# A transformer layer on one core: attention, gates and Fourier map ordered on every engine by one plan

## The chip, the cores and the metric

The kernel runs on one core of one Trainium2 chip. A core has a matrix engine (PE; its weight loads are listed as PEld), a vector engine (DVE), an activation engine (ACT), a general engine (POOL) and a queue engine (SP) that here only issues DMAs. Each engine takes its instructions in the order in which they stand in the program and waits at semaphores for the others. The metric is device time of the whole layer in microseconds (us), lower is better.

## The reference

One layer: a mixer of two branches (attention and a Fourier branch) merged by sigmoid gates, then a squared-ReLU MLP. All inputs are float32, 1024 latent tokens, 256 context tokens, width 1024, 8 heads.

```python
hx = modulate(rmsnorm(x, norm1_g[l]), sh1, sc1)          # hc: the same for the context
fx, qlx, kvlx, krx, gx = split_proj(hx @ w_in[l])        # 512 | 256 | 128 | 32 | 2 x 1024 gates
kx, vx = mla_kv(kvlx, krx, kv_norm_g[l], w_kvb[l], k_gain[l], rope)
qx = mla_q(qlx, q_norm_g[l], w_qb[l], q_gain[l], rope)
# 8 heads, 96 numbers for q and k, 64 for v; 1024 queries over 1024 + 256 keys
att_x = latent_attention(qx, jnp.concatenate([kx, kc], axis=1), jnp.concatenate([vx, vc], axis=1))
g = jax.nn.sigmoid(gx + b_gate)
y = g_f * (fourier_mix(fx) @ w_fourier) + g_a * (att_x @ w_mla_o)
x = x + g1 * (y @ w_out)
h2 = modulate(rmsnorm(x, norm2_g[l]), sh2, sc2)
x = x + g2 * jnp.square(jax.nn.relu(h2 @ w_up)) @ w_down
```

## The kernel before

Tokens lie along the free dimension in two halves of 512. A float32 product is made of three matmuls: each operand is split into a rounded high part (ACT copies it) and a low part (DVE subtracts), and PE multiplies high-high, high-low and low-high. So nearly every operand costs one ACT and one DVE instruction.

The program has three parts.

The **front**, up to the first head of attention: projections, norms, the q and k vectors of all heads (kept in DRAM), v, the Fourier transforms over positions, and the first 8 of 16 gate blocks. Each step is a task with an engine, an assumed duration, dependencies and buffers. `plan` (line 263) is a list scheduler: it takes the task that can start first by its assumed durations, and for equal starts the one with the smaller priority number. The 128 pieces of the first 8 gates (three matmuls each, `g_piece`) have the lowest rank and fill PE's gaps. All five engines issue in the plan's order. The front also holds 24 sums `ada_dot` that make later modulation numbers; 12 of them run on DVE at line 928, of low rank too. `first_head` makes q and k of head 0 and the row maxima of its first query half: 12 matmuls, 12 DVE maxima (line 1431), then a diagonal matrix of the negative maxima (line 1436, DVE) that PE turns into a row (`row`) and ACT copies under q, so that the score matmul subtracts the maximum.

**Attention** has 160 steps: 8 heads x 2 query halves x 10 key blocks. A step is three score matmuls (`score`), two exponentials on ACT (a float16 high part and a float32 one), a low part `pp` on DVE for each third step and on POOL else, and 4 + 4 float16 matmuls with v (`weigh`: 129 columns for the high part, 65 for the low one). The next head's q and k are loaded, multiplied by their norm on POOL (`hat`), split, and their row maxima made (`smax`, line 1529). The other 8 gates are spread over the steps (`gates_plan`), the Fourier map (`fmap_plan`) over the last 20 and beyond. Each action is filed with a time in steps (`at`), and `advance` makes them in order of time. Only PE is bound to that order (`manual_schedule(engines={PE})`); DVE, ACT, POOL and SP are ordered by the framework's own scheduler. The front's plan is written out in full before attention's first action. `k_tiles(1)`, which writes a row of ones into the second set of k tiles on POOL, and two small DVE products for later (`ax2`, `g1h`) stand between.

The **rest**, from the merge to the MLP, is a second plan, again ordered on all engines.

Buffers are rings: 58 of 2 KB per partition (`u`), 8 for short use (`t`), 5 for `pp`; in PSUM two banks each for maxima (`p0`), scores (`p1`), v products (`p2`), gates and Fourier map (`p4`).

Of the kernel before, what the change touches and what calls it, by code (L numbers as in the profile page):

```python
# [23 lines left out]
KB = 8  # L24
# [7 lines left out]
def hybrid_layer_kernel(ctx, tc, xT, ctxT, cvec, cctx, adaw, smalls, w_in4, w_in, w_qb, w_kvk, w_kvv, w_fo, w_f64,  # L32
# [216 lines left out]
    def lag(d, eng):  # L249
# [7 lines left out]
                              r"u2_|x_\d|c22_|c12_|c21_")  # L257

    def on_port(n):
        eng, dur = tasks[n][:2]  # L260
        return eng == "POOL" and dur > 0.3 or eng == "DVE" and not free_of_port.match(n)

    def plan(pre=None):
# [22 lines left out]
        while ready:  # L286
            best = None
            for n in ready:
                eng, dur, _, _, deps, new, _ = tasks[n]
                st = max([end[d] + lag(d, eng) for d in deps], default=0.0)  # L290
                st = max(st, free.get(eng, 0.0), free.get("port", 0.0) if on_port(n) else 0.0)
                want = {}
                for tag, _ in new:
                    want[tag] = want.get(tag, 0) + 1
                for tag, m in want.items():
                    if len(slots[tag]) < m:
                        break
# [681 lines left out]
    def c_add(j):  # L979
        tt(C["q", j][:, 0], C["q", j][:, 0], C["q", j][:, 1], ALU.add, nc.gpsimd)  # L980
# [63 lines left out]
    def alt_cast():  # L1044
        DT["a"] = Tm((1, 514), F32R)
# [196 lines left out]
    def g_piece(i, hf, k):  # L1242
        key = f"G{i}{hf}"

        def run():
# [73 lines left out]
    load("altl", 0.1, alt_load, ("q16",), (("t", "altr"),))  # L1319
    op("altc", "ACT", 0.55, alt_cast, ("altl",), (("t", "alta"),), ("altr",))  # L1320
# [75 lines left out]
    def first_head():  # L1396
        op("hk", "POOL", 3.0, lambda: k_tiles(0), ("ds1",), tuple(("u", f"hxk{i}") for i in range(6)))
# [11 lines left out]
        for c in range(2):  # L1409
# [7 lines left out]
            op(f"hqt{c}", "SP", 0.02, tiles, ("ds1",), (("u", f"hxq{c}h"), ("u", f"hxq{c}l")))  # L1417
# [1221 lines left out]
```

## Time and profile before

| | us |
|---|---|
| runs | 1485.41, 1482.95, 1488.93 (median 1485.41) |
| profiled execution | 1487.4 |
| its span (first to last instruction) | 1485.6 |
| front, to the first head's maxima | 0 to about 320 |
| end of the front and start of attention | about 320 to 364 |
| attention | about 339 to 707 |
| rest | from about 720 |
| PE busy | 1430.8 (96%) |
| DVE / ACT / POOL busy | 1117.8 (75%) / 789.0 (53%) / 346.4 (23%) |

Matmuls are pipelined, so PE counts as busy from the first start to the last end of a dense row. A stretch is full when the granted clock (PEclk) is 1.00 and matmuls follow without a gap, as in the rest (3245 matmuls in 763.6 us); a half clock shows as 0.50. The profile's rows name instructions by the program's tile names, as out<-in; line 79 is the matmul helper, 93 an elementwise helper, 99 the activation helper.

### The profile page before, as it was taken

To read this page: it belongs to the slowest core of one execution; us is meant where nothing else is said; L and a number is where in the kernel's file an instruction comes from. 1 tells how busy PE (TensorE), PEld (TensorE's weight loads), DVE (VectorE), ACT (ScalarE), POOL (GpSimd) and SP (SyncE) were. 2 spreads that over 40 slices of the span, in tenths; PEclk is the share of its full clock that TensorE was granted. 3 is DMA by queue.
4 is the path that set the end of the run, shared out by engine and by line. 5 is a ranking of instruction groups with operands and counts; after the bars stand their busy time and mean duration, and the time that the engine had idled before them with its cause. 6 is when DMAs were issued, how large, how long until landed. Compare 5 with 4: busy or idle time off the path is not lost. (4 is left out here: it accounts for less than half of the span.)

```text
span 1485.6 us, 20465 instructions
## 1 busy us (share of the span) xinstructions
PE 1430.8 (96%) x7208; PEld 1125.5 (76%) x7208; DVE 1117.8 (75%) x1763; ACT 789.0 (53%) x1287; POOL 346.4 (23%) x277
## 2 busy tenths in 40 slices
PE   8999999996999999999999999999999999999998
PEld 7767667874777777776887787888888788888887
DVE  4898786668776867786866888876666888877885
ACT  5654757653777777777433474444444443333431
POOL 0010653613554537355321200000000110100000
PEclk9999998997999999999999999999999999999999
DMA  9413455575222312213748556564444883536232
GB/s 339 160 45 129 149 169 169 179 227 172 65 85 76 91 49 80 68 50 105 246 146 276 164 175 207 199 227 156 151 140 154 288 288 120 199 100 206 92 127 100
DMA packets 103520, 229.09 MB, mean 154 GB/s; under 512 B 12765, under 2 KB 15877, under 8 KB 103418
## 3 DMA queue, kind: packets, MB, share of 16 engines
q1 hardware_dynamic: 103418, 227.80, 46.3%
q8 instruction: 56, 0.92, 0.3%
q14 instruction: 46, 0.38, 0.1%
HBM read 171.12 MB, written 56.61 MB: 153 GB/s over the span
## 5 line engine op out<-in xcount | busy, mean ns | idle before, releaser
L79 PE MATMUL ps<-u,wh 128*128 128x512 f32 (+1 forms) x1760 | 557.5, 398 | 2.2 <-DVE u L96 1.0
L79 PEld LDWEIGHTS ps<-u,wh 128*128 128x128 f32 x1760 | 326.8, 191 | 77.2 <-issue 4.0
L79 PE MATMUL ps<-u,wl 128*128 128x512 f32 (+2 forms) x880 | 344.6, 392 | 0.0
L79 PE MATMUL ps<-u,u 96*128 96x512 f32 (+4 forms) x862 | 250.6, 406 | 21.2 <-DVE mx L1529 8.9
L79 PEld LDWEIGHTS ps<-u,u 96*128 96x128 f32 (+3 forms) x862 | 158.3, 194 | 64.5 <-DVE mx L1529 14.0
L79 PEld LDWEIGHTS ps<-u,wl 128*128 128x128 f32 x880 | 167.6, 190 | 37.2
L93 POOL TENSOR_TENSOR u<-u,u 96x512 f32<-96x512 f32 (+1 forms) x34 | 52.0, 1536 | 530.6 <-DVE t L93 323.7
L99 ACT ACTIVATE wh<-wr 128x1024 fp32r<-128x1024 f32 (+1 forms) x108 | 94.6, 881 | 136.9 <-DMA wr<-d 103.0
L93 POOL TENSOR_TENSOR pp<-t,pp 128x512 f16<-128x512 f32 x106 | 126.1, 1192 | 144.9 <-ACT t L99 53.1
L79 PE MATMUL ps<-ab,pp 128*128 128x129 f16 (+2 forms) x1504 | 154.4, 238 | 4.9 <-ACT pp L99 2.8
L99 ACT ACTIVATE pp<-ps,lnps 128x512 f16<-128x512 f32 x160 | 109.4, 684 | 69.9 <-PE ps L79 68.4
L1529 DVE TENSOR_REDUCE mx<-ps 128x1 f32<-128x512 f32 (+1 forms) x180 | 105.2, 595 | 53.0 <-PE ps L79 52.0
L93 DVE TENSOR_TENSOR wl<-wr,wh 128x1024 fp32r<-128x1024 f32 (+1 forms) x108 | 125.7, 1169 | 18.8 <-ACT wh L99 18.6
L79 PE MATMUL ps<-u,ab 128*128 128x512 f32 (+4 forms) x516 | 120.8, 384 | 2.0 <-DVE t L1208 1.3
L93 DVE TENSOR_TENSOR u<-u,u 128x512 f32<-128x512 f32 (+5 forms) x139 | 106.0, 782 | 19.2 <-ACT u L99 16.7
L99 ACT ACTIVATE t<-ps 128x512 f32<-128x512 f32 (+6 forms) x102 | 52.7, 522 | 118.2 <-PE ps L79 107.6
L79 PEld LDWEIGHTS ps<-u,ab 128*128 128x128 f32 (+1 forms) x516 | 92.5, 189 | 24.6 <-DVE t L1208 2.2
L99 ACT ACTIVATE t<-ps,lnps 128x512 f32<-128x512 f32 x160 | 108.1, 681 | 0.0
L99 ACT ACTIVATE t<-t 128x512 f32<-128x512 f32 (+4 forms) x138 | 84.2, 619 | 44.3 <-DVE t L93 32.5
L99 ACT ACTIVATE u<-u 128x512 fp32r<-128x512 f32 (+4 forms) x120 | 72.0, 611 | 65.9 <-POOL u L93 35.1
L79 PE MATMUL ps<-ab,u 128*128 128x512 f32 x240 | 91.6, 395 | 0.0
L79 PE MATMUL ps<-wh,u 128*128 128x512 f32 x232 | 91.2, 396 | 0.0
(194 smaller groups left out, 2136.4 us busy)
## 6 DMA issues: line engine op xcount, KB each, us to landing
d<-t SPq DMA_DIRECT2D x135, 256.0 KB, 2.4
wr<-d SPq DMA_DIRECT2D x56, 512.0 KB, 3.5
wr<-in_w_up_dram SPq DMA_DIRECT2D x39, 512.0 KB, 4.9
u<-in_adaw_dram SPq DMA_DIRECT2D x64, 256.0 KB, 4.3
u<-in_w_dn_dram SPq DMA_DIRECT2D x64, 256.0 KB, 6.8
ab<-in_adaw_dram SPq DMA_DIRECT2D x24, 512.0 KB, 5.9
t<-d SPq DMA_DIRECT2D x48, 256.0 KB, 4.2
wr<-in_w_in_dram SPq DMA_DIRECT2D x22, 512.0 KB, 5.5
```

The costliest lines, as they stand in the source:

```text
L79: return nc.tensor.matmul(o, lhsT=l, rhs=r, start=start, stop=stop, **k)
L93: (eng or nc.vector).tensor_tensor(out=o, in0=a, in1=b, op=op)
L99: nc.scalar.activation(out=o, in_=i, func=f, **k)
L1529: nc.vector.reduce_max(out=x["mx"][:, qb, kc:kc + 1], in_=p[:, :n], axis=AX.X)
```

## The change

Attention, gates 8 to 15 and the Fourier map become tasks of the front's plan, which now orders all five engines up to the end of the Fourier map. The names of PE's tasks: `S_n` scores, `H_n` and `W_n` the products of the high and low parts with v, `mm` a maximum's matmul, `mr` the row of maxima, `gp` a gate piece, `fm` the Fourier map; `E_n`, `X_n` are the exponentials, `L_n` the low part, `red_m` a maximum, `md` the diagonal.

- These tasks are "late": their priorities are 1000 plus twice the step, and they do not lengthen the front's own chains. Equal starts go to the front's tasks first; what can start earlier goes earlier.
- `either` lets the plan choose DVE or POOL for a task: low parts, the multiplications of q and k, two sums of the Fourier map's weights and one of its result, four sums of the context's squares. Counted in the two programs, 50 instructions of 282 move from POOL to DVE: 20 low parts, 15 multiplications of q and k, 15 sums.
- The norms of k are loaded per block and no longer once per head (788 SP DMAs for 781). After the v products one `scalar_tensor_tensor` does what a `tensor_scalar` and a `tensor_tensor` did: 32 `tensor_scalar` go.
- `k_tiles(1)` is a task without a dependency on the modulation sums; `ax2` and `g1h` follow the plan.
- The one-row table `alt` of the position transform is loaded after the third Fourier block and not after the q vectors.
- The gates' and q/k tiles are tracked as buffers; PE's matmuls are the same in number and shape (8372 rows with weight loads).

```diff
     def plan(pre=None):
...
-                tail[n] = tasks[n][1] + max([depth(m) + lag(n, tasks[m][0]) for m in succ[n]], default=0.0)
+                tail[n] = tasks[n][1] + max([depth(m) + lag(n, tasks[m][0]) for m in succ[n] if m not in late_tasks],
+                                            default=0.0)
...
+                for eng, dur in either.get(n, (tasks[n][:2],)):
+                    st = max([end[d] + lag(d, eng) for d in deps], default=0.0)
+                    st = max(st, free.get(eng, 0.0), free.get("port", 0.0) if on_port(n, eng, dur) else 0.0)
...
+                        key = (st + (GAP if prio[n] >= 1e6 else 0.0), prio[n], st + dur)
...
-        op(f"gp{n}", "PE", 3 * M, run, (f"gp{n - 1}" if n else "F30b", f"G{i}l0", f"G{i}l1"),
+        n = KB * gseq.index((i, hf)) + k
+        s = GS + (n - 16 * NGB + 0.5) * (GE - GS) / (16 * (16 - NGB))
...
+        op(f"gp{n}", "PE", 3 * M, run, (f"gp{n - 1}" if n else "F30b", f"G{i}l0", f"G{i}l1",
+                                        *((f"S_{int(s) - GA}",) if s >= GA and n >= 16 * NGB else ())),
...
+           1e6 + n if n < 16 * NGB else P0 + W * s)
...
-    load("altl", 0.1, alt_load, ("q16",), (("t", "altr"),))
+    load("altl", 0.1, alt_load, ("F20b",), (("t", "altr"),))
...
-    order, ends = plan()
-    for t, fn in order:
-        at(t, fn)
-    with tc.manual_schedule(engines=MANUAL):
-        advance(1e6)
...
-    k_tiles(1)
...
+    def late(name, eng, dur, fn, deps=(), new=(), use=(), t=0.0):
+        late_tasks.add(name)
+        task(name, eng, dur, P0 + W * t, fn, *deps, new=new, use=use)
+
+    def late_any(name, dve, pool, fn, deps=(), new=(), use=(), t=0.0):
+
+        late(name, "DVE", dve, lambda: fn(nc.gpsimd if tasks[name][0] == "POOL" else nc.vector), deps, new, use, t)
+        either[name] = (("DVE", dve * SCALE["DVE"]), ("POOL", pool * SCALE["POOL"]))
...
+        late(f"S_{n}", "PE", 3 * M + 0.03, score,
+             (qdep(h, c, "l"), kdep(h, kc, "l"), "hsc" if n < 10 else f"mc{hc}", *((f"S_{n - 1}",) if n else ())),
+             (("p1", f"sp{n}"),), (f"qh{hc}h", f"qh{hc}l", f"kt{b}{kc}", f"kt{b}{3 + kc}"), n)
+        late(f"E_{n}", "ACT", 0.61, exp_h, (f"S_{n}",), (("pp", f"pp{n}"),), (f"sp{n}",), n + 0.3)
+        late(f"X_{n}", "ACT", 0.61, exp_f, (f"E_{n}",), (("t", f"pf{n}"),), (f"sp{n}",), n + 0.35)
+        late_any(f"L_{n}", 0.65, 1.16, lambda e: e.tensor_tensor(out=x["pp"][:, 1], in0=x["f"], in1=x["pp"][:, 0],
+                                                                 op=ALU.subtract),
+                 (f"X_{n}",), (), (f"pp{n}", f"pf{n}"), n + 0.9)
...
+    late("hk1", "POOL", 3.0, lambda: k_tiles(1), ("hk",), tuple(("u", f"kt1{i}") for i in range(6)), (), -8)
...
+    order, ends = plan()
+    with tc.manual_schedule(engines=MANUAL):
+        for _, fn in order:
+            fn()
+    stt(ax2, adam[:, 32:40], 1.0, sm[:, N2G:N2G + 8], ALU.add, ALU.mult)
+    nc.vector.tensor_scalar_mul(out=g1h, in0=adam[:, 16:24], scalar1=0.5)
```

**Where the order differs.** Place 1 is PE at the row of the first maxima (`onesr`) and the first scores. Before (`wh_3287`, `wl_3288` are gate weights, `u_2685` is k's third block, `u_2661` its first, `u_2683` q):

```order
L79 MATMUL ps_3306<-u_902,wh_3287 128x512
L79 MATMUL ps_3306<-u_903,wh_3287 128x512
L79 MATMUL ps_3306<-u_902,wl_3288 128x512
L79 MATMUL ps_3306<-u_907,wh_3287 128x512
L79 MATMUL ps_3198<-u_2685,u_2661 128x256
L79 MATMUL ps_3306<-u_908,wh_3287 128x512
L79 MATMUL ps_3306<-u_907,wl_3288 128x512
L79 MATMUL ps_3216<-t_3210,onesr 128x512
L79 MATMUL ps_3329<-u_2661,u_2683 128x512
L79 MATMUL ps_3329<-u_2662,u_2683 128x512
L79 MATMUL ps_3329<-u_2661,u_2686 128x512
```

Between the last maximum (`u_2685`, 256 columns) and the row stand two matmuls of a gate piece here, and nothing between the row and the first score. After (`wh_3201` are the weights of the ninth gate, `u_2681`, `u_2691`, `u_2679` are head 0's k and q, `u_2747` and `u_2924` to `u_3134` q and k of the next maxima):

```order
L79 MATMUL ps_3242<-u_910,wh_3201 128x512
L79 MATMUL ps_3242<-u_911,wh_3201 128x512
L79 MATMUL ps_3242<-u_910,wl_3202 128x512
L79 MATMUL ps_3263<-t_3250,onesr 128x512
L79 MATMUL ps_3242<-u_915,wh_3201 128x512
L79 MATMUL ps_3242<-u_916,wh_3201 128x512
L79 MATMUL ps_3242<-u_915,wl_3202 128x512
L79 MATMUL ps_3273<-u_2924,u_3134 128x512
L79 MATMUL ps_3242<-u_919,wh_3201 128x512
L79 MATMUL ps_3242<-u_920,wh_3201 128x512
L79 MATMUL ps_3242<-u_919,wl_3202 128x512
L79 MATMUL ps_3283<-u_2691,u_2679 128x512
```

Behind the last maximum's matmul of head 0 (it stands 18 rows ahead of the row now) five gate pieces and two matmuls of the next maxima stand before the row, and two more pieces and another such matmul between the row and the first score.

Place 2 is DVE at the same spot; the reductions `mx` are head 0's maxima, `ISA ... sil` is one half of an `ada_dot`, `t_3210` and `t_3250` are the diagonal. Before:

```order
L1431 TENSOR_REDUCE mx<-ps_3188 128x1
L1431 TENSOR_REDUCE mx<-ps_3192 128x1
L928 ISA t_3200,adam<-u_3126,sil,adam 128x512
L928 ISA adam 128x1
L1431 TENSOR_REDUCE mx<-ps_3198 128x1
L928 ISA t_3205,adam<-u_3133,sil,sm 128x512
L928 ISA adam 128x1
L1435 TENSOR_REDUCE m_3208<-mx 128x4
L93 TENSOR_TENSOR wl_4061<-wr_3912,wh_4060 128x512
L93 TENSOR_TENSOR t_3210<-nid,m_3208 128x512
L928 ISA t_3214,adam<-u_3140,sil,adam 128x512
L928 ISA adam 128x1
```

Three halves of `ada_dot` stand here among the last maxima and behind the diagonal. After:

```order
L1443 TENSOR_REDUCE mx<-ps_3220 128x1
L93 TENSOR_TENSOR wl_3202<-wr_3166,wh_3201 128x512 x2
L1443 TENSOR_REDUCE mx<-ps_3227 128x1
L93 TENSOR_TENSOR u_2684<-u_3144,u_2681 96x256
L1447 TENSOR_REDUCE m_3248<-mx 128x4
L93 TENSOR_TENSOR t_3250<-nid,m_3248 128x512
L1564 TENSOR_REDUCE mx<-ps_3231 128x1
L1564 TENSOR_REDUCE mx<-ps_3252 128x1
L93 TENSOR_TENSOR u_2928<-u_3183,u_2925 96x512
L93 TENSOR_TENSOR u_2929<-u_3103,u_2926 96x256
L96 SCALAR_TENSOR_TENSOR adam<-pr,sm 128x1
L932 ISA t_3275,adam<-u_3129,sil,sm 128x512
```

The `ada_dot` halves that stood among the maxima and on both sides of the diagonal stand behind it now.

Place 3 is the start of the position transform. ACT before; `1x514` is the cast of `alt`, which PE's first 1-row matmuls of the transform read, `wh_2295` the weights of the fifth gate:

```order
L99 ACTIVATE wh_2295<-wr_2232 128x512
L99 ACT_TABLE_LOAD
L99 ACTIVATE g_2298<-ps_2234,bg_84 128x512
L99 ACTIVATE wh_2295<-wr_2232 128x512
L99 ACTIVATE t_2309<-t_2174 1x514
L99 ACT_TABLE_LOAD
L99 ACTIVATE t_2301<-t_2300 128x256
```

The cast stands between the gate weights' activations, just before the transform. ACT after:

```order
L99 ACTIVATE t_1238<-u_878 128x512
L99 ACTIVATE t_1239<-u_893 128x512
L99 ACTIVATE u_1263<-t_1236 1x514
L99 ACTIVATE t_1268<-t_1267 128x512
L99 ACTIVATE t_1269<-t_1268 128x512
L99 ACTIVATE t_1305<-ps_1244 128x512
```

The cast has moved some hundred rows ahead. PE there, after (`ones` are the context's sums, `ab_1062` the transform; before, no piece of `wh_2295` stood ahead of the transform):

```order
L79 MATMUL ps_2300<-t_2282,ones 128x256
L79 MATMUL ps_2300<-t_2287,ones 128x256
L79 MATMUL ps_2312<-u_866,wh_2297 128x512
L79 MATMUL ps_2312<-u_867,wh_2297 128x512
L79 MATMUL ps_2312<-u_866,wl_2298 128x512
L79 MATMUL ps_2300<-t_2292,ones 128x256
L79 MATMUL ps_2300<-t_2303,ones 128x256
L79 MATMUL ps_2322<-u_2153,ab_1062 128x258
```

A piece of the fifth gate pair stands now between the context's sums.

## Rows read from the trace of the kernel before

**Rows 1.** The page: span; busy us (share) xinstructions of each engine.
```profile
span 1485.6 us, 20465 instructions
...
PE 1430.8 (96%) x7208; PEld 1125.5 (76%) x7208; DVE 1117.8 (75%) x1763; ACT 789.0 (53%) x1287; POOL 346.4 (23%) x277
```

**Rows 2.** Stages: length, busy us (xcount) by engine, PEclk, DMA share, GB/s.
```profile
237.50:262.00 24.50, 22.16 (x107) 17.08 (x108) 15.03 (x30) 18.31 (x39) 5.30 (x5) 0.79 0.42 128
262.00:320.00 58.00, 58.00 (x286) 47.63 (x284) 34.61 (x64) 35.66 (x78) 28.36 (x29) 1.00 0.64 212
320.00:364.00 44.00, 28.42 (x112) 20.02 (x110) 36.05 (x73) 15.39 (x26) 13.08 (x11) 0.77 0.59 184
364.00:640.00 276.00, 266.76 (x1951) 203.56 (x1949) 209.19 (x408) 201.95 (x336) 142.75 (x118) 1.00 0.23 72
640.00:722.00 82.00, 77.41 (x530) 59.43 (x531) 61.59 (x111) 55.00 (x98) 42.39 (x33) 0.94 0.37 116
722.00:1485.60 763.60, 756.41 (x3245) 609.65 (x3243) 575.76 (x770) 323.13 (x465) 53.38 (x34) 1.00 0.53 178
```

**Rows 3.** Timeline of PE, 320 to 362: start, us, instruction [idle before <-releaser].
```profile
322.61 0.77 PE L79 MATMUL ps<-u,u 96*128 96x512 f32 x1 [2.26 <-DVE mx L1431]
...
337.63 0.80 PE L79 MATMUL ps<-t,onesr 128*128 128x512 f32 x1 [3.64 <-DVE t L93]
...
352.62 0.40 PE L79 MATMUL ps<-ab,pp 128*128 128x129 f16 x4 [2.83 <-ACT pp L99]
...
359.51 2.08 PE L79 MATMUL ps<-u,u 96*128 96x512 f32 x4 [2.40 <-DVE mx L1529]
```

**Rows 4.** Matmuls by form, 320 to 364: xcount, busy us, mean ns, idle before.
```profile
L79 PE MATMUL ps<-u,u 96*128 96x256 f32 x7 | 2.2, 309 | 0.5 <-DVE mx L1529 0.5
L79 PE MATMUL ps<-ab,pp 128*128 128x129 f16 x16 | 1.4, 221 | 2.8 <-ACT pp L99 2.8
...
L79 PE MATMUL ps<-ab,pp 128*128 128x65 f16 x12 | 0.8, 233 | 0.0
```

**Rows 5.** DVE by form, 322 to 364.
```profile
L928 DVE CUSTOM_DVE_ANT_0 t<-u,sil,sm 128x512 bf16<-128x512 f32 x8 | 6.7, 835 | 0.0
L928 DVE CUSTOM_DVE_ANT_0 t<-u,sil,adam 128x512 bf16<-128x512 f32 x8 | 6.3, 792 | 0.0
```

**Rows 6.** Timeline of POOL, 309 to 351.
```profile
332.56 1.04 POOL L93 TENSOR_TENSOR u<-ones 1x512 fp32r<-1x512 f32 x1 [23.36 <-DVE adam L928]
...
349.52 1.81 POOL L93 TENSOR_TENSOR u<-u,u 96x512 f32<-96x512 f32 x1 [12.49 <-DMA u<-d]
```

**Rows 7.** Timeline of all engines, 242.5 to 245.
```profile
242.67 0.61 ACT L99 ACTIVATE t<-t 1x514 fp32r<-1x514 f32 x1
...
242.80 0.69 DVE L93 TENSOR_TENSOR wl<-wr,wh 128x512 fp32r<-128x512 f32 x1 [0.52 <-ACT wh L99]
...
243.33 0.50 PE L79 MATMUL ps<-t,u 1*128 1x258 f32 x2 [2.30 <-ACT t L99]
```

**Rows 8.** DVE by form, 364 to 640.
```profile
L93 DVE TENSOR_TENSOR pp<-t,pp 128x512 f16<-128x512 f32 x42 | 32.7, 778 | 6.3 <-ACT t L99 5.9
L93 DVE TENSOR_TENSOR u<-u,u 96x512 fp32r<-96x512 f32 x25 | 26.2, 1048 | 8.0 <-ACT u L99 7.7
...
L1647 DVE TENSOR_SCALAR rs<-rs,inv 128x2 f32<-128x2 f32 x26 | 9.3, 402 | 0.0
```

**Rows 9.** POOL by form, 364 to 640.
```profile
L93 POOL TENSOR_TENSOR pp<-t,pp 128x512 f16<-128x512 f32 x86 | 101.9, 1187 | 122.2 <-PE ps L79 36.5 <-ACT t L99 33.5 <-DVE mx L1529 17.7
```

**Rows 10.** DVE by form, 262 to 322.
```profile
L93 DVE TENSOR_TENSOR u<-u,u 96x512 fp32r<-96x512 f32 x4 | 2.7, 692 | 2.2 <-ACT u L99 2.2
```

**Rows 11.** Waits of PE, 364 to 640: us in total, times, longest.
```profile
PE ps L79 <- DVE mx L1529: 5.7, 10, 0.9
PE ps L79 <- DVE t L93: 1.6, 2, 1.1
PE ps L79 <- ACT u L99: 1.4, 1, 1.4
```

More of the change, by code (lines that the diff above doesn't have):

```diff
@@ L1299, in hybrid_layer_kernel @@
         op(f"ca{j}", "POOL", 0.65, lambda j=j: c_add(j), (f"cs{j}",), (), (f"cxq{j}",))
+        either[f"ca{j}"] = (("DVE", 0.38), ("POOL", 0.68))
     def delayed(seq, one, stat, d):
@@ L1396, in first_head @@
     def first_head():
-        op("hk", "POOL", 3.0, lambda: k_tiles(0), ("ds1",), tuple(("u", f"hxk{i}") for i in range(6)))
+        op("hk", "POOL", 3.0, lambda: k_tiles(0), ("ds1",), tuple(("u", f"kt0{i}") for i in range(6)))
         op("nid", "DVE", 0.2, lambda: nc.vector.tensor_scalar_mul(out=nid, in0=ident, scalar1=-1.0))
@@ new lines, in hybrid_layer_kernel, with hat, run_ld @@
+    NS = len(steps)
+    TT5, RD5, AC5, GP5 = 0.63, 0.58, 0.56, 1.25
+    FS, FE, FP = 140, 182, 121
+    def hat(key, n, loads, h, l, deps, ld, hdep, hnew, uses, ts):
+        x = {}
+        d = 1.0 if n == HF else 0.55
+        one = n == NC_
+        def run_ld():
+            if one:
+                w = U((96, 2, n))
+                x["w"], x["r"] = w[:, 0], w[:, 1]
+            else:
+                x["w"], x["r"] = U((96, n)), U((96, n))
+            loads(x)
+        keys = (f"{key}w",) if one else (f"{key}w", f"{key}r")
+        late_load(f"{key}ld", 1.0 if one else 1.2, run_ld, (*deps, *ld), tuple(("u", k) for k in keys), ts[0])
+        late_any(f"{key}m", TT5 * d, GP5 * d, lambda e: e.tensor_tensor(out=x["w"], in0=x["w"], in1=x["r"], op=ALU.mult),
+                 (f"{key}ld",), (), keys, ts[1])
+        late(f"{key}h", "ACT", AC5 * d, lambda: act(h(), x["w"], AF.Copy), (f"{key}m", *hdep), hnew, (keys[0], *uses), ts[2])
+        late(f"{key}l", "DVE", TT5 * d, lambda: tt(l(), x["w"], f32(h()), ALU.subtract), (f"{key}h",), (),
+             (keys[0], *uses), ts[3])
@@ new lines, in smax @@
+        t += dt * 12
+        late(f"md{k}", "DVE", 0.9, diag, ("nid", *(f"red_m{k}{i}" for i in range(12))), (("t", f"mdg{k}"),), (), t)
+        late(f"mr{k}", "PE", M, row, (f"md{k}",), (("p0", f"mrp{k}"),), (f"mdg{k}",), t + 0.2)
+        late(f"mc{k}", "ACT", AC5, lambda: act(qhs[h][c][96:97, :], x["p"][96:97, :], AF.Copy), (f"mr{k}",), (),
+             (f"mrp{k}", f"qh{k}h"), t + 0.3)
+    pps = {}
+    pvs = {}
+    att = {}
+    at_d = [[D([P, HF]) for _ in range(2)] for _ in range(4)]
@@ new lines, in att_split, with high, at_load, ld @@
+    def att_split(cb, c, get, dep, key, t):
+        def high():
+            attTh[cb][c], attTl[cb][c] = U(dt=F32R), U(dt=F32R)
+            act(attTh[cb][c], get(), AF.Copy)
+        late(f"aT{cb}{c}h", "ACT", AC5, high, (dep,), (("u", f"pm{cb}{c}h"), ("u", f"pm{cb}{c}l")), (key,), t)
+        late(f"aT{cb}{c}l", "DVE", TT5, lambda: tt(attTl[cb][c], get(), f32(attTh[cb][c]), ALU.subtract), (f"aT{cb}{c}h",),
+             (), (key,), t)
+    def at_load(cb, c, t):
+        x = {}
+        def ld():
+            x["r"] = U()
+            nc.sync.dma_start(out=x["r"], in_=at_d[cb][c])
+        late_load(f"aL{cb}{c}", 0.75, ld, (f"trd{cb}{c}", *step(t)), (("u", f"aLr{cb}{c}"),), t)
+        att_split(cb, c, lambda: x["r"], f"aL{cb}{c}", f"aLr{cb}{c}", t + 4)
```

577 lines of the change are left out of this document (271 added, 306 removed).

## The prediction

> **What bounds the kernel now.** I read the page first: PE is busy 96% of 1485.6 us and no other engine more than 75% [rows 1]. PE's matmuls are the same before and after, so the change can only fill, or open, stretches in which PE stands still or runs at its lower clock. The windows by stage say where these are [rows 2]. In the rest (722 to the end) 3245 matmuls take 756.41 of 763.60 us, 0.233 us each, at a granted clock of 1.00: full, and not touched. From 262 to 320 PE is busy in all of 58.00 us: full as well. Four places are left:
>
> - The end of the front, 320 to 364: only 112 matmuls in 44.00 us, busy 28.42, clock 0.77.
> - The start of the position transform, 237.5 to 262: 22.16 of 24.50, clock 0.79.
> - Attention, 364 to 640: 266.76 of 276.00, clock 1.00.
> - Its tail, 640 to 722: 77.41 of 82.00, clock 0.94.
>
> Next I read PE's timeline in the worst one [rows 3]. The reader is to see four stops with three different releasers: DVE's maxima (2.26 us), DVE's diagonal (3.64), ACT's first exponential (2.83), DVE's maxima of the next block (2.40). Behind such stops the granted clock falls from 2.4 to 1.2 GHz for a while, which is why 0.77 stands there while the full stretches have 1.00. Then DVE and POOL there, to see why the releasers are late [rows 5, 6].
>
> **Term 1, the end of the front.** What its work is worth: of the 112 matmuls 7 are of 256 columns and 28 short products with v [rows 4], so 77 are long. 77 x 0.233 = 17.9, 7 x 0.117 = 0.8, and the 28 lie between 28 x 0.05 = 1.4 (129 and 65 columns for 512, mean 97, so 0.19 x 0.233 = 0.044, rounded up) and 28 x 0.137 = 3.8 (266.76 us over 1951, attention's mean, which holds long ones too). Work 20.1 to 22.5 us, so of 44.00 us 21.5 to 23.9 are lost, by idle time (44.00 - 28.42 = 15.6) and by clock.
>
> Why they are lost: 16 halves of `ada_dot` take 6.7 + 6.3 = 13.0 us of DVE there, 0.8 each [rows 5]. In the order before they stand among the last maxima and on both sides of the diagonal, that is, on the chain maxima, minimum, diagonal, row, score. POOL stands 23.36 us behind the modulation sums, because `k_tiles(1)` follows them, and then 12.49 us for the loads of the next head [rows 6], so the next maxima come late too. Before, two gate matmuls were all that PE had between the last maximum and the row.
>
> What the change does: the halves stand behind the diagonal (place 2), `k_tiles(1)` does not follow the sums, and the ninth gate is at hand. Between the last maximum's matmul and the row PE has 5 pieces and 2 matmuls, 15 x 0.233 + 2 x 0.117 = 3.7 us; between row and score 2 pieces and 1 matmul, 7 x 0.233 = 1.6. That stands against a stop of 3.64 [rows 3] that itself held about 2 halves (1.6 us) which now come later. So the stop should be gone. The exponential's stop (2.83) can be filled with pieces of gates as well. The halves do not vanish: 13.0 us of DVE move into attention, where I count them below.
>
> Value: -18.5 of some 22.5, which leaves one stop like 2.40 with the clock behind it. Bounds: -23.9 (all of it), and -8 (only the stops 3.64 and 2.26 = 5.9 go, with a fifth of the 0.23 x 44.00 = 10.1 us of clock, 2.0).
>
> **Term 2, the position transform.** Its first 1-row matmul starts at 243.33 after 2.30 us of waiting for the cast of `alt`, made 242.67 to 243.28 [rows 7]. Idle 2.34 and clock 0.21 x 24.50 = 5.1 make 7.4 us. The cast now stands some hundred rows earlier on ACT, so that wait goes. What is late next: a gate piece now stands ahead of the transform, and the low part of such weights ended at 242.80 + 0.69 = 243.49 before [rows 7]. If that DVE row is as late as it was, PE waits about 2.5 us for it instead and nothing is won. Bounds: -7.4, and +3 (this wait and a second like 2.30, less what the one removed saved). I take -4, between nothing and all.
>
> **Term 3, attention.** Idle 9.2 us, and three releasers make 8.7 of it: maxima 5.7 in 10 stops of at most 0.9, diagonals 1.6, a copy of ACT 1.4 [rows 11]. The plan can put a maximum ahead of a low part. But DVE gets more to do. Over 320 to 722 it is busy 36.05 + 209.19 + 61.59 = 306.8 of 402 us [rows 2], 76%, the 13.0 us of halves included. 20 low parts at 778 ns are +15.6 [rows 8], 30 products and sums at 692 ns +20.8 [rows 10], 32 `tensor_scalar` at 402 ns -12.9 [rows 8]: 330 us. PE needs 402 - 25 = 377 us by my terms, so DVE is at 88%. POOL loses 20 x 1.187 = 23.7 us of low parts [rows 9] beside the products, and nothing waits longer for it. The 7 added DMAs I cost at nothing: the DMA engines are busy 0.23 of attention [rows 2], and if that cover were gone POOL would wait for them first, as it does now (12.49 us [rows 6]). Bounds: -9.2 (all), +10 (each of the 10 stops waits for one low part more on DVE, 0.8 us, with 2 for clock). I take -4.
>
> By the row, a product on two SBUF operands takes 1048 ns on DVE in attention and 692 in the stage before, though POOL is busy about half of either (142.75 of 276.00 and 28.36 of 58.00) [rows 2, 8, 10]. The Trainium skill (SBUF — State Buffer, Who interferes with whom) says that DVE's second pair of SBUF ports is GpSimd's only one, and that the later of two such operations waits for all of the earlier. Its page Perfetto Trace Analysis (Optimizing Scalar/DVE Operations) adds that moving work between the two might for that reason not help. By that rule a low part on DVE takes away a POOL operation that had held DVE up: in the kindest case the 23.5 us that DVE gains above come to nothing, 307 of 377 is 81%, and rival C below would have 0.08. The equal share of POOL beside unequal times speaks neither for it nor against it, so the sum stays with the rows.
>
> **Term 4, the tail.** Idle 4.6 us, clock 0.06 x 82.00 = 4.9: 9.5 lost [rows 2]. The Fourier map's weights are now loaded and split in one order with the last scores, and gates may be used up earlier, since some fill term 1. Bounds -9.5 and +5 (idle doubled). I take -2.5, half of the idle time.
>
> **Sum.** -18.5 - 4 - 4 - 2.5 = -29.0. The profiled execution took 1487.4 us, 1.8 of it around the span, and so 1458.4. It lay 2.0 above the median of the runs, 1485.41; I take 1458. All best bounds together give 1437, all worst 1497.
>
> **Rivals.**
> - A. The short stops go as well: one order for all engines puts every maximum and every copy in time, and the terms 3 and 4 come out at their best bounds: -18.5 - 4 - 9.2 - 9.5 = -41.2, 1446 us. For it: no stop of attention is longer than 1.4 [rows 11], small against a piece. Against: DVE at 88%.
> - B. Only the stops by DVE go at the end of the front; the first exponentials and the next maxima stay late, because the loads of the next head are behind others in SP's queue (12.49 us of POOL's idle time are a DMA's [rows 6]), and the other terms give nothing: -8, 1479 us.
> - C, slower. DVE becomes the bound in attention. Each of the 15 blocks of maxima behind the first (8 heads x 2 halves) stops PE as long as the longest such stop now, 2.40 [rows 3]: +36 on 1458, 1494 us. It decides when DVE's 330 us become 377, so if its operations get 14% longer or gather in front of the diagonals. For it: low parts took 1048 and 778 ns there, and every engine follows one order, so that a late one holds up all behind it. Against: only 5.7 us of maxima's stops at 76%.
> - D. The change does not do what it says: the times that the plan assumes differ from the chip's, the stops move to other instructions and PE loses as much as before. 1485 us.
>
> **Chances.** Forecast 0.48 (its own range 1448 to 1470: term 1 between -10 and -23.9, the others by half of their bounds), A 0.18, B 0.15, C 0.12, D 0.07. 0.5% is 7.4 us, about what a measurement of this kernel tells from no change. Faster, below 1478: forecast, A, and 0.06 of B, which lies at this edge, 0.72. Same: 0.09 of B and D, 0.16. Slower, above 1493: C, 0.12. The range 1440 to 1486 takes in the forecast, most of A, B and most of D; C and the best part of A are left out, some 0.2.
>
> **What would show it.** Term 1: between 300 and 350 us the granted clock stays at 1.00 and no stop of PE at the row exceeds 1 us; POOL has no idle time of 23 us behind `adam`; the `ada_dot` halves lie in attention. Term 2: no wait of PE for a 1x514 activation, and the stage around the transform at clock 1.00; wrong if PE waits there for `wl`. Term 3: DVE's busy share over attention 85 to 90% with stops by maxima under 6 us; wrong, towards C, if these exceed 20 us. Term 4: clock 1.00 up to the Fourier map's last matmul. The forecast is wrong as a whole if PE's stages sum to the same idle time as before, or if the rest changes its 763 us.

## The result and the profile after

The changed kernel takes 1461.17 us (median of 4 runs, 1457.53 to 1464.61) for 1484.18: a ratio of 0.9845, 95% interval 0.9804 to 0.9886, so 23 us less (17 to 29). The forecast was 1458 us. The profiled execution took 1464.6 us, 3.4 above the median, with a span of 1462.8 for 1485.6, and it is this difference of 22.8 us that the stages below explain.

The first view is that of the stages (length, busy us and xcount of PE, PEld, DVE, ACT, POOL, then PEclk, DMA share, GB/s) [rows 2]. Attention begins and ends earlier, so its stages are cut at 620 and 700.

```profile
237.50:262.00 24.50, 22.02 (x121) 16.98 (x120) 18.36 (x35) 18.22 (x40) 4.38 (x3) 0.93 0.51 161
262.00:320.00 58.00, 54.15 (x257) 43.16 (x256) 38.01 (x53) 35.74 (x73) 31.41 (x32) 0.97 0.47 146
320.00:364.00 44.00, 43.79 (x250) 33.00 (x250) 38.09 (x77) 27.50 (x49) 12.10 (x11) 1.00 0.52 164
364.00:620.00 256.00, 251.21 (x1809) 184.72 (x1808) 208.62 (x405) 187.59 (x312) 105.23 (x88) 0.99 0.30 93
620.00:700.00 80.00, 78.50 (x562) 59.55 (x561) 68.43 (x137) 58.47 (x105) 17.40 (x14) 1.00 0.41 131
700.00:1462.80 762.80, 754.75 (x3239) 608.22 (x3237) 574.84 (x765) 322.53 (x464) 51.79 (x34) 1.00 0.53 178
```

Between 320 and 364 us PE now makes 250 matmuls for 112, at a clock of 1.00 for 0.77: the hole is gone. The stage before it, full in [rows 2] (58.00 of 58.00), has one now (54.15). The rest is as it was.

Second, the timeline of PE (start, us, instruction, idle time before and its releaser), with all stops of 1 us and more from 237 to 620 [rows 3]:

```profile
240.71 1.74 PE L79 MATMUL ps<-t,ones 128*128 128x256 f32 x4 [2.48 <-DVE t L93]
...
288.11 1.42 PE L79 MATMUL ps<-u,u 128*128 128x512 f32 x5 [1.49 <-DVE u L93]
295.79 2.93 PE L79 MATMUL ps<-u,u 128*128 128x512 f32 x6 [2.09 <-DVE ab L93]
...
438.01 1.57 PE L79 MATMUL ps<-u,u 96*128 96x256 f32 x6 [1.07 <-DVE mx L1564]
...
444.67 0.50 PE L79 MATMUL ps<-u,u 96*128 96x512 f32 x1 [1.80 <-DVE mx L1564]
```

None lies at the first row of maxima or the first score. The first stands where PE had waited for the cast of `alt`, the next two where it had not waited, the last two are attention's.

Stages of equal clock times do not hold equal work, so a third view is needed. In it each matmul counts with the usual distance to its successor for its shape, 1361.1 us in every run, and a stage ends when a certain sum is reached (200, 240, 280, 340, 560, 620 us of work). What a stage takes above its work is lost; some 4 us behind the last matmul stand in no row. Each column is one profiled execution; where two kernels have one order on PE (after and e10; e7, e11 and e12) the columns still differ by 1 to 3 us. With the median distance of each shape instead (1375.9 us) the changes by stage shift by up to 1.1 us.

| lost us | before | after | e1 | e2 | e3 | e5 | e6 | e7 | e8 | e9 | e10 | e11 | e12 |
|---|---|---|---|---|---|---|---|---|---|---|---|---|---|
| start (to 235) | 34.8 | 36.0 | 34.6 | 34.1 | 34.6 | 35.7 | 35.6 | 35.0 | 35.3 | 35.0 | 34.4 | 33.9 | 35.9 |
| transform (to 285) | 10.1 | 7.0 | 4.9 | 4.6 | 5.5 | 6.5 | 7.2 | 5.2 | 7.2 | 6.9 | 4.9 | 5.1 | 5.2 |
| after it (to 330) | 4.7 | 7.6 | 7.4 | 9.5 | 5.9 | 2.5 | 1.8 | 2.5 | 5.0 | 5.6 | 5.8 | 4.4 | 4.6 |
| end of front (to 417) | 27.2 | 4.7 | 17.1 | 14.4 | 9.6 | 25.1 | 29.4 | 4.7 | 6.8 | 27.8 | 4.7 | 3.9 | 3.9 |
| attention (to 659) | 22.0 | 24.7 | 19.8 | 17.4 | 22.3 | 23.0 | 22.2 | 20.7 | 26.2 | 19.9 | 20.0 | 20.8 | 22.5 |
| its tail (to 730) | 11.2 | 6.6 | 6.7 | 6.6 | 6.6 | 11.3 | 11.2 | 6.8 | 8.7 | 6.6 | 6.6 | 6.6 | 6.6 |
| rest | 10.3 | 11.0 | 9.2 | 9.4 | 9.1 | 10.1 | 10.5 | 10.5 | 8.4 | 8.0 | 8.2 | 8.3 | 8.3 |

(In brackets where the stage ends in the kernel before; e1 to e12 are the experiments.) The change by stage: start +1.2, transform -3.1, after it +2.9, end of the front -22.5, attention +2.7, tail -4.6, rest +0.7. So nearly the whole gain is the hole at the end of the front. The stage behind the transform and attention seem to pay a little back; each by itself is no larger than what columns of one order differ by.

Last, DVE by form (xcount, busy us, mean ns, idle before) from 364 to 620 [rows 8]:

```profile
L1633 DVE TENSOR_TENSOR pp<-t,pp 128x512 f16<-128x512 f32 x45 | 34.6, 770 | 4.0 <-ACT t L99 3.4 <-issue 0.5
L93 DVE TENSOR_TENSOR u<-u,u 96x512 fp32r<-96x512 f32 x23 | 20.6, 895 | 0.0
...
L932 DVE CUSTOM_DVE_ANT_0 t<-u,sil,adam 128x512 bf16<-128x512 f32 x8 | 7.1, 891 | 0.0
L932 DVE CUSTOM_DVE_ANT_0 t<-u,sil,sm 128x512 bf16<-128x512 f32 x8 | 6.9, 875 | 0.0
```

16 halves of modulation sums, 14.0 us, lie in attention now; the low parts of q and k take 895 ns for 1048. And from 262 to 322 [rows 10], where the four took 692 ns:

```profile
L93 DVE TENSOR_TENSOR u<-u,u 96x512 fp32r<-96x512 f32 x5 | 12.9, 2586 | 3.7 <-DMA d<-t 3.7
```

### The profile page after: what moved, and what is told of

Read it like the earlier page. It is cut to its first block, busy times and chain, and to the rows that moved or that the text cites. A ratio compares the mean times of both kernels' runs of the same rounds, so it can differ in the third digit from the quotient of the medians.

```text
span 1462.8 us, 20410 instructions
## 1 busy us (share of the span) xinstructions
PE 1425.7 (97%) x7208; PEld 1114.0 (76%) x7208; DVE 1132.6 (77%) x1781; ACT 788.4 (54%) x1287; POOL 280.2 (19%) x227
## 5 line engine op out<-in xcount | busy, mean ns | idle before, releaser
L79 PE MATMUL ps<-u,wh 128*128 128x512 f32 (+2 forms) x1760 | 551.6, 395 | 2.4 <-DVE u L96 1.0
L79 PEld LDWEIGHTS ps<-u,wh 128*128 128x128 f32 x1760 | 323.4, 189 | 76.2 <-issue 3.8
L79 PE MATMUL ps<-u,u 96*128 96x512 f32 (+5 forms) x874 | 264.1, 411 | 13.6 <-DVE mx L1564 3.0
L79 PEld LDWEIGHTS ps<-u,u 96*128 96x128 f32 (+4 forms) x874 | 156.6, 193 | 49.8 <-DVE mx L1564 4.9
L79 PE MATMUL ps<-ab,pp 128*128 128x65 f16 (+2 forms) x1504 | 167.4, 237 | 0.1
L1633 POOL TENSOR_TENSOR pp<-t,pp 128x512 f16<-128x512 f32 x86 | 103.9, 1214 | 188.1 <-ACT t L99 78.0
L93 POOL TENSOR_TENSOR u<-u,u 128x512 f32<-128x512 f32 (+1 forms) x20 | 29.9, 1500 | 515.0 <-DVE t L93 323.4
L93 DVE TENSOR_TENSOR u<-u,u 128x512 f32<-128x512 f32 (+3 forms) x139 | 109.3, 806 | 7.5 <-DMA d<-t 3.7
L79 PEld LDWEIGHTS <-pp 128*128 128x128 f16 x1280 | 62.5, 98 | 55.1 <-issue 32.4
```

The costliest lines, as they stand in the source:

```text
L79: return nc.tensor.matmul(o, lhsT=l, rhs=r, start=start, stop=stop, **k)
L93: (eng or nc.vector).tensor_tensor(out=o, in0=a, in1=b, op=op)
L1633: late_any(f"L_{n}", 0.65, 1.16, lambda e: e.tensor_tensor(out=x["pp"][:, 1], in0=x["f"], in1=x["pp"][:, 0], op=ALU.subtract), (f"X_{n}",) ...
```

## Experiments

Ratios are to the kernel before, run on the same chip; the changed kernel has 0.9845. Each interval is 0.2 to 0.5% to either side, 3 to 8 us.

### What made the hole: e1, e2, e3, e4, e6, e9

Theory H, that of the prediction: modulation sums on DVE stood on the chain of the first maxima. Rival F: PE only lacked work to fill the hole. **e1**, sums ahead of attention again:

```diff
-        ... (f"ad_{i - 2}",) if i >= 2 else (ADT,), 1e5 + i)
+        ... (f"ad_{i - 2}",) if i >= 2 else (ADT,), 900.0 + i)
```

> The changed kernel, but its low-rank modulation sums (ada_dot) get a rank ahead of attention's tasks, so that halves of them stand on DVE again among the last maxima of head 0, before and behind the diagonal. Theory H (the halves on the chain maxima-diagonal-row-score made the hole of 44 us): PE's idle time between 300 and 364 us, 0.5 us in the changed kernel, comes back to 6 us or more, and the time is 1468 to 1476 for 1461. Rival F (PE only lacked work to fill the hole, and gates and the next maxima now stand there whatever DVE does): PE stays full there, idle under 2 us, and the time is 1461 plus or minus 3.

Measured: 1464.87 us, 0.9883 (0.9848 to 0.9919), between the two. PE's idle time between 300 and 364 us is 5.94, about what H expected, and in its timeline stops come back:

```profile
331.14 0.72 PE L79 MATMUL ps<-u,u 96*128 96x256 f32 x2 [2.55 <-DVE mx L1443]
...
362.54 0.49 PE L79 MATMUL ps<-t,onesr 128*128 128x512 f32 x1 [1.82 <-DVE mx L1564]
```

The end of the front loses 17.1 for 4.7, as H says, but attention loses 19.8 for 24.7, where DVE has the sums behind it. By the ratios the time is 5.6 us longer (0.0038 of 1484), less than half of the 12.4 us lost here, and the two intervals overlap. **e2**, e1 and the second k tiles behind the sums:

```diff
-    late("hk1", "POOL", 3.0, lambda: k_tiles(1), ("hk",), ...
+    late("hk1", "POOL", 3.0, lambda: k_tiles(1), ("hk", "ad_22", "ad_23"), ...
```

> As the run before, and the rows of ones of the second k tiles wait for the last two modulation sums as well, as they did before the change, so head 1's k and q come late. Theory H: two thirds of the gain of term 1 are lost, 1474 to 1484. Rival F: gates fill the place, 1461 to 1466.

1465.35 us, 0.9886 (0.9851 to 0.9920): no more than e1, as F expected, though the stage still loses 14.4. **e3**, no later gate ahead of the first score:

```diff
-   *((f"S_{int(s) - GA}",) if s >= GA and n >= 16 * NGB else ())),
+   *((f"S_{max(int(s) - GA, 0)}",) if n >= 16 * NGB else ())),
```

> The changed kernel, but no piece of the gates 8 to 15 may stand ahead of the first score; the sums stay behind the diagonal. Between the last maximum and the row stand 2 gate pieces and 2 maxima (about 1.9 us of PE) for 5 and 2 (3.7 us). Theory H: the chain itself is short now, the stops at the row and the score stay under 1 us each, 1461 to 1464. Rival F: PE stops at the row and at the first score for 2 us each and falls to the lower clock behind it, 1467 to 1473.

1462.88 us, 0.9879 (0.9835 to 0.9922). Stops at the row (1.08, a little over H's 1 us) and the score (0.35) are small, as H expected; 4.9 us more are lost in the stage and 2.4 won in attention. The time can't be told from the changed kernel's.

**e4** was to take the sums alone out of the chain of the kernel before.

> The kernel before with one thing changed: the last 8 modulation sums (16 halves, 13 us of DVE) may only start behind the copy of the first row of maxima. Theory H: the stops of PE at the maxima (2.26) and at the diagonal (3.64) shrink to 1 us or less; the next maxima still come late, since the second k tiles' rows of ones follow the sums; 1476 to 1481 for 1484. Rival F: PE has nothing else to do there, so the hole only moves: 1482 to 1487.

1495.40 us, 1.0101 (1.0050 to 1.0152), slower, against both. It tells nothing of the sums: the new dependency lengthened the front's chains and with them the ranks of its tasks, so that PE's order differs from 73 us on, long before these sums. Its trace is not compared by stage: that execution took 1505.71 us, 10 above the median. **e6** has the dependency left out of the chains' lengths, and PE's order is the one of before but for a few rows at 333 us:

```diff
-   ... (f"ad_{i - 2}",) if i >= 2 else (ADT,), 1e5 + i)
+   ... (f"ad_{i - 2}", *(("hsc",) if i >= 16 else ())) if i >= 2 else (ADT,), 1e5 + i)
-   ... for m in succ[n]], default=0.0)
+   ... for m in succ[n] if n != "hsc" or m[:3] != "ad_"], default=0.0)
```

> The kernel before with the last 8 modulation sums (16 halves on DVE) behind the copy of the first row of maxima, and no other task moved. Theory H (the halves on the chain make the hole): the two stops of PE at the maxima and at the diagonal go, 1474 to 1478 for 1482 to 1484. Rival F (without other work to fill it, the hole only moves behind the first scores, where the next maxima wait for the same 13 us of DVE): 1480 to 1486, and PE loses 20 us or more between 300 and 364 us as before.

1484.61 us, 1.0008 (0.9988 to 1.0028): nothing. PE's timeline shows why:

```profile
330.24 0.50 PE L79 MATMUL ps<-t,onesr 128*128 128x512 f32 x1 [1.33 <-DVE t L93]
...
339.00 0.80 PE L79 MATMUL ps<-u,u 96*128 96x512 f32 x1 [3.66 <-DVE mx L1530]
...
356.15 2.50 PE L79 MATMUL ps<-u,u 96*128 96x512 f32 x5 [4.82 <-ACT u L99]
```

The stop at the row shrinks from 3.64 [rows 3] to 1.33, but the next maxima wait longer (3.66 for 2.40 [rows 3]), and PE waits 4.82 for a copy of ACT. The stage loses 29.4 for 27.2: the hole has only moved. H, as the cause by itself, falls. **e9** undoes the three parts of e1 to e3 at once, and holds the next maxima back too, with one plan on all engines still:

```diff
     (e1, e2 and e3, and)
+    late(f"mm{k}{i}", ..., *(("ad_22", "ad_23") if (h, c) == (0, 1) else ()), ...
```

> The changed kernel with a wall between front and attention: the modulation sums rank ahead of attention, and the second k tiles, the next maxima and (till the first score) the gates 8 to 15 wait as in the first three runs, all at once; the order is still one plan on all engines. Theory F (any one of sums, maxima and gates is filled by the others; the hole of 27 us comes back when all of them are kept out): PE loses 20 us or more at the end of the front, 1474 to 1486. Rival O (the hole went because all engines follow one order, whatever work is let in): the losses stay under 15 us there, 1462 to 1468.

1473.90 us, 0.9935 (0.9916 to 0.9954): 13 us slower than the changed kernel, at the lower edge of what F expected, and the end of the front loses 27.8 us, as before the change (27.2). PE's timeline, and the stages there:

```profile
332.80 0.79 PE L79 MATMUL ps<-t,onesr 128*128 128x512 f32 x1 [2.42 <-DVE t L93]
...
371.63 0.77 PE L79 MATMUL ps<-u,u 96*128 96x512 f32 x1 [2.35 <-DVE mx L1564]
```
```profile
328.00:364.00 36.00, 30.97 (x170) 21.00 (x168) 31.15 (x71) 16.99 (x28) 4.70 (x4) 0.89 0.53 184
364.00:415.00 51.00, 45.56 (x269) 31.73 (x269) 39.02 (x79) 30.08 (x51) 17.52 (x15) 0.81 0.22 65
```

So F holds in the main: with all of this work kept out the hole is back, its stops and its lower clock, and O falls. Four kernels tell the two causes apart. Without work to fill it the stage loses 27.8 us with the sums on the chain (e9) and 29.4 with them off it (e6, in the program of before). With such work it loses 17.1 with the sums on the chain (e1) and 4.7 with them off (the changed kernel). So the place of the sums counts only when there is work to fill with, and then it is worth up to 12.4 us of the stage. Maxima were held back only together with the rest, so what they are worth alone is not shown.

### The position transform: e5

**e5** is the kernel before with the early load and cast of `alt` alone:

```diff
-    load("altl", 0.1, alt_load, ("q16",), (("t", "altr"),))
-    op("altc", "ACT", 0.55, alt_cast, ("altl",), (("t", "alta"),), ("altr",))
+    load("altl", 0.1, alt_load, ("F20b",), (("t", "altr"),))
+    op("altc", "ACT", 0.55, alt_cast, ("altl",), (("u", "alta"),), ("altr",))
```

> The kernel before with the early load and cast of the one-row table alone (after the third Fourier block, its cast kept in the large ring). Theory: the wait of 2.30 us and the lower clock behind it go, 1476 to 1480 for 1482 to 1484, with the stage 237 to 262 at a clock over 0.95. Rival: PE waits there for the weights' low part of DVE instead, the clock stays at 0.8, 1482 to 1486.

1476.50 us, 0.9949 (0.9928 to 0.9969): 5 to 11 us faster by the early load and cast alone. The wait for the cast is gone, the largest left in the place is

```profile
238.97 1.38 PE L79 MATMUL ps<-t,ones 128*128 128x256 f32 x4 [1.04 <-POOL t L93]
```

and the clock of the stage 0.93 for 0.79, a little under the 0.95 expected. The table shows 3.6 us of the gain in the transform, 2.2 behind it and 2.1 at the end of the front.

### What DVE pays: e8, e10, e7, e11, e12

**e8** undoes the choice of engine for low parts and for the products of q and k (it also lets a pair of sums of the v products follow each other, not shown here):

```diff
+        if name[0] in "KQ":
+            either[name] = either[name][1:]
+        if name[0] == "L":
+            either[name] = (either[name][int(name[2:]) % 3 > 0],)
```

> The changed kernel with the choice between DVE and POOL undone for low parts (each third on DVE) and for the products of q and k (all on POOL), as before the change; the plan still orders all. Theory P (the choice is worth little, since DVE's operations get longer while POOL works): DVE's busy time in attention falls by less than 10 us, PE loses 22 to 27 us in attention as with the choice, 1460 to 1465. Rival G (the choice is what keeps attention short): low parts come late from POOL, PE waits for them, 1468 to 1476.

1464.22 us, 0.9852 (0.9811 to 0.9893): Theory P. DVE in its three stages from 320 to 700 us:

```profile
320.00:364.00 44.00, 42.04 (x243) 30.96 (x242) 35.39 (x71) 25.23 (x44) 13.27 (x11) 1.00 0.44 144
364.00:620.00 256.00, 249.70 (x1811) 182.99 (x1810) 201.72 (x374) 188.80 (x315) 139.22 (x111) 1.00 0.30 93
620.00:700.00 80.00, 75.91 (x544) 57.83 (x543) 68.56 (x131) 57.40 (x102) 30.64 (x23) 1.00 0.38 121
```

That is 305.7 us; with the choice it is 38.09 + 208.62 + 68.43 = 315.1. With 35 operations more in the whole program, of 0.7 us and more each, DVE is busy only 9.4 us longer here, and 4.8 over the whole run (1132.6 for 1127.8). What else it does gets shorter. In e8, from 364 to 620:

```profile
L1637 DVE TENSOR_TENSOR pp<-t,pp 128x512 f16<-128x512 f32 x39 | 34.1, 873 | 0.9 <-ACT t L99 0.8
...
L93 DVE TENSOR_TENSOR wl<-wr,wh 128x512 fp32r<-128x512 f32 x12 | 12.0, 1010 | 0.1
```

and in the changed kernel 770 ns for 873 and 745 for 1010. **e10** shortens the sums on DVE (it leaves out most of each):

```diff
-   ... in0=x[j], in1=sl(j), ...
+   ... in0=x[j][:, :8], in1=sl(j)[:, :8], ...
```

> The changed kernel in its own order, with the modulation sums on DVE taken over 8 of 512 columns (leaves out the rest of these sums): 24 halves on DVE at 0.1 to 0.2 us for 0.8. Theory B (the halves that left the front's end cost attention time on DVE): PE's loss in attention falls from 24.7 to 18 to 20 us, 1454 to 1457 for 1461. Rival (attention hides them, its losses come from its own chains): 1459 to 1463.

1451.64 us, 0.9781 (0.9748 to 0.9814), faster than B expected. A half still takes 0.31 to 0.35 us, and attention's loss falls from 24.7 to 20.0, as B expected. But of the 13.0 us between the two profiles 8.3 stand in stages in which no shortened half lies, so these are differences between executions. And e7, whose plan differs, loses 20.7 with all halves at full length. So B is likely and not shown.

**e7** takes POOL's products out of the two places where new stops stand (and leaves the new dependencies out of the chains' lengths, as in e6):

```diff
-   ... (f"ad_{i - 2}",) if i >= 2 ...
+   ... (f"ad_{i - 2}", *(("cx3",) if i in (3, 4, 5) else ("hq1l",) if 8 <= i < 12 else ())) if i >= 2 ...
```

> The changed kernel, with POOL's products of seven modulation sums moved out of two stretches: those of sums 3 to 5 behind the context's sums, those of 8 to 11 behind q's last low part of head 0. Theory L (a DVE product of two SBUF operands waits as long as POOL works without a gap): the low parts of head 0's q and k, 3.92 and 5.62 us long in the changed kernel, take 0.7 to 1.4 us, PE's stops of 1.49 and 2.09 us at 288 and 296 go, and the time is 1454 to 1459 for 1461. Rival (these low parts are late for their loads, and POOL has no part in it): the stops stay, 1460 to 1464.

1452.71 us, 0.9785 (0.9754 to 0.9816), 8 to 9 us faster than the changed kernel (the intervals overlap a little), and the best ratio among the kernels that leave nothing out, with e11's next to it. What it removes is seen in the changed kernel, on DVE and then on POOL:

```profile
287.98 5.62 DVE L93 TENSOR_TENSOR u<-u,u 96x512 fp32r<-96x512 f32 x1
```
```profile
287.66 1.54 POOL L93 TENSOR_TENSOR u<-u,u 96x512 f32<-96x512 f32 x1 [0.76 <-DVE u L93]
289.15 1.30 POOL L93 TENSOR_TENSOR u<-u,sil 128x512 f32<-128x512 f32 x1
290.38 0.18 POOL L1158 MEMSET ab<- 128x16 f16 x1
290.45 1.30 POOL L93 TENSOR_TENSOR u<-u,sil 128x512 f32<-128x512 f32 x1
291.69 0.18 POOL L1158 MEMSET ab<- 128x16 f16 x1
291.75 1.30 POOL L93 TENSOR_TENSOR u<-u,sil 128x512 f32<-128x512 f32 x1
```

POOL works without a gap from 287.66 to 293.05, and a DVE product of 0.68 us that starts beside it ends at 293.60. In e7 DVE's low parts from 262 to 322 are, and the stage is:

```profile
L93 DVE TENSOR_TENSOR u<-u,u 96x512 fp32r<-96x512 f32 x7 | 4.6, 677 | 0.0
```
```profile
262.00:320.00 58.00, 56.97 (x267) 45.39 (x267) 39.92 (x67) 38.57 (x78) 32.37 (x32) 1.00 0.54 167
```

677 ns for 2586, and the stops at 288 and 296 are gone. Attention loses 4.0 us less as well, in a plan that differs there. **e11** adds four POOL products without a gap to e7, each of one tile with itself:

```diff
+            for _ in range(4 if key == "hq1" else 0):
+                tt(x["r"], x["r"], x["r"], ALU.mult, nc.gpsimd)
```

> The kernel of the run with POOL's products moved (1452.7), with four products of 96x512 more on POOL, without a gap, behind the product of head 0's second q half; they change a tile that is read no more, and no other instruction moves. Theory L: DVE's products of two SBUF operands that come due in these 5 us (282 to 288) wait to their end, one of them takes 3 us or more for 0.7, PE stops for 2 to 4 us at 285 to 300, and the time is 1455 to 1461. Rival (DVE shares the port instruction by instruction): none takes over 2 us, 1452 to 1454.

1451.50 us, 0.9792 (0.9760 to 0.9825): no slower. DVE, then POOL:

```profile
284.33 0.69 DVE L93 TENSOR_TENSOR wl<-wr,wh 128x512 fp32r<-128x512 f32 x1 [1.24 <-ACT wh L99]
285.70 0.77 DVE L93 TENSOR_TENSOR wl<-wr,wh 128x512 fp32r<-128x512 f32 x1 [0.68 <-ACT wh L99]
...
287.59 2.87 DVE L93 TENSOR_TENSOR u<-u,u 96x512 fp32r<-96x512 f32 x1
```
```profile
282.11 5.25 POOL L93 TENSOR_TENSOR u<-u 96x512 f32<-96x512 f32 x4
287.31 0.16 POOL L1159 MEMSET ab<- 128x16 f16 x1
287.37 2.54 POOL L93 TENSOR_TENSOR u<-u,sil 128x512 f32<-128x512 f32 x2
```

The four do not keep DVE out; the two products of the sums behind them do (2.87). Theory L in its simple form, any row of POOL work, is wrong. But the four are no row without a gap, since each reads what the one before wrote. Two of them by themselves:

```profile
283.23 1.04 POOL L93 TENSOR_TENSOR u<-u 96x512 f32<-96x512 f32 x1
```
```profile
284.35 1.57 POOL L93 TENSOR_TENSOR u<-u 96x512 f32<-96x512 f32 x1
```

The first ends at 284.27, 0.08 us before the next starts. DVE's product of 284.33 starts in this gap, and it is POOL's that takes longer (1.57 for 1.04). DVE's next one comes 0.22 us before that ends, and takes 0.77. None came due in the middle of one of the four, so e11 doesn't show that a product of one tile with itself lets DVE in. **e12** lets the four read two tiles:

```diff
-                tt(x["r"], x["r"], x["r"], ALU.mult, nc.gpsimd)
+                tt(x["r"], x["r"], x["w"], ALU.mult, nc.gpsimd)
```

> The run before with one thing changed: the four products added on POOL read two tiles each (the dead one times q's half, which ACT and DVE read beside it) and not one tile twice. In the run before no DVE product was held up beside these four (0.69 and 0.77 us between 284 and 287), while one beside the products of the modulation sums behind them took 2.87. Theory L2 (a POOL product of two tiles keeps DVE's products out, one that reads a tile twice does not): a low part of weights or of k and q that comes due between 282 and 288 takes 2 us or more, and the time is 1452 to 1458. Rival (these DVE products aren't kept out by POOL's products of 96x512, only by those of 128x512 with the modulation's vector): they take 0.7 to 0.8 us again, 1450 to 1454.

1454.76 us, 0.9809 (0.9781 to 0.9837). DVE by form from 286 to 289.2:

```profile
L93 DVE TENSOR_TENSOR wl<-wr,wh 128x512 fp32r<-128x512 f32 x2 | 3.0, 1498 | 1.2 <-ACT wh L99 1.1
```

Neither number came: not 2 us and more, not 0.7 to 0.8, but 1.5 for 0.73 in e11. Each of the two waits out one POOL product, and not the whole row of them. In this row too each product uses the result of the one before, and a gap stands between them (the first of these two ends at 287.14):

```profile
285.83 1.31 POOL L93 TENSOR_TENSOR u<-u,u 96x512 f32<-96x512 f32 x1
```
```profile
287.21 1.62 POOL L93 TENSOR_TENSOR u<-u,u 96x512 f32<-96x512 f32 x1
```

In the changed kernel's row the products are independent of one another, and the second starts at 289.15, 0.05 us before the end of the first. All traces together bear the gap out (counted over the 14 traces of this case). DVE's products of two SBUF operands and 512 columns came due in the middle of a POOL product 725 times. Where POOL's next product started after the end of that one (505 times), none waited for a second. Where it started before that end (220 times), 28 did. So without a gap a long wait can come, and with one it did not; what decides without a gap is not shown.

## Why the prediction was right, point by point

**What bounds.** Right: the gain lies in PE's holes, and the rest kept its 763 us (762.8 with a cut 6 matmuls later).

**Term 1, -18.5: measured -22.5**, within its bounds. The size was right and the reason given for it only in part. The step that failed is to explain the loss by the halves on the chain: taking them off alone brought nothing (e6), and putting them back cost 12 us there but some 5 in the time, within the noise (e1). What fills the hole is that the plan may put attention's maxima, gates and scores among the front's last tasks (e9). The prediction counted this work (5 pieces and 2 matmuls between maximum and row, 3.7 us) against one stop of 3.64, and should have had it as the cause of the whole. The one stop that it left in place did not stay. Its signs held: clock 1.00 and no stop at the row, the halves in attention or behind the diagonal, and POOL's wait of 23.36 us [rows 6] gone.

**Term 2, -4: measured -3.1** in the profiles, and -2.9 to -5.5 in six more of the same order there (e1 to e3 and e8 to e10: 4.6 to 7.2 for 10.1). Alone it brought 5 to 11 us (e5). What is late next was named wrong: not the weights' low part, but the context's sums on DVE, at 240.71 after 2.48 us. That this wait is as long as the 2.5 us that the prediction gave for the other is chance, and with it something was won. The stage's clock is 0.93, not the 1.00 forecast.

**Term 3, -4: measured +2.7** in this profile, and -1.3 to +0.5 in those of e7, e11 and e12, which have all sums in attention as well. This step was wrong: no 4 us were won. The stops by maxima did shrink, as forecast:

```profile
PE ps L79 <- DVE mx L1564: 3.0, 3, 1.8
```

from 5.7 [rows 11]. But the 13 us of halves came to attention (up to 4.7 us of loss by e10), and attention's loss is only in part made of stops that the list of waits names. The prediction counted the halves in DVE's sum and gave them no price on PE. That this price made the difference is likely and not shown.

DVE's own sum was too high: 330 us forecast, 315.1 measured, 83% of 380 us for 88%. Moving work from POOL to DVE cost about a third of its length (e8: 9.4 us for 26.0 forecast), because what remains on DVE gets shorter. That is part of the way to where the rule that the prediction weighed would have it. By the Trainium skill (SBUF — State Buffer, Who interferes with whom) the later of the two engines waits for the shared ports. The 5.62 us and e7 agree with it; so does e11, where POOL's product came second and took 1.57 us for 1.04.

**Term 4, -2.5: measured -4.6.** The term took half of the idle time and nothing of the clock, and this was too little: from 620 to 700 the clock is 1.00 for 0.94, as its sign asked, and 1.50 us of idle time stay. In e8 the tail loses 8.7 for 6.6, but there some halves of the sums lie in it too, so what the choice of engine is worth here is open.

**What no term had:** +2.9 us behind the transform, a new hole in a stage that had been full [rows 2]. The order at place 2 showed DVE's rows alone; POOL's products of the sums beside head 0's low parts were not looked at. The plan's assumed times do not let the two engines' products overlap (`on_port`), but in the trace they do. e7 shows them to be the cause, and 5 us can be had back.

**Rivals.** A, B and D did not come. C's bound was not reached (DVE at 83%), though its way, DVE late by what holds it up, is what cost the stage behind the transform. Against the forecast stand -4.0 and -2.1 in terms 1 and 4, +6.7 in attention, +2.9 behind the transform, +0.9 in term 2 and +1.9 in stages that were not to change, together +6.3 on -29.0. That the misses of both signs nearly cancel, and the time comes out near 1458, is luck. The median is nearer to the forecast than that, since this profiled execution lies 3.4 us above it.

## What to carry to other kernels

When a hole on the bounding engine follows a chain on others, ask first which work the order allows into it, and only then what stands on the chain: here the hindrances of e1 to e3 cost the time some 5 to 6 us each, within the noise, the wall of e9 13, and a shorter chain without filler only moved the hole. A task moved off a critical place may have to be paid for where it lands, so give it a price there on the bounding engine. And look at what the general engine does beside the vector engine's short operations: a row of its products without a gap can make 0.7 us into 5.6, which ordering them apart gives back.

## What the runs showed of the hardware

A DVE product of two SBUF tiles waited for up to four POOL products and two memsets on end (5.62 us for 0.68), and for 2.87 us beside two of them (e11). Where each POOL product used the result of the one before, 0.07 to 0.08 us stood between them; a DVE product that came due in the middle waited for one of them (1.5, e12), and one that started in the gap for none (0.69, e11), while POOL's took 1.57 for 1.04. So whether POOL's products leave a gap, and not its busy share alone, decides in these traces how long DVE can be kept waiting.
